# Hybrid decoder step on one core: the mixer's gate pairs summed on VectorE, and the sample output's steps moved apart

## The chip, the cores and the metric

The kernel runs on one core of a Trainium2 chip. The metric is the device time of one launch in microseconds (us), the median of several runs. The profile is one execution under the hardware profiler.

The core has TensorE (PE: matmuls; PEld is its weight load), VectorE (DVE), ScalarE (ACT) and GpSimd (POOL). SyncE (SP) issues most DMA transfers. Each engine runs its own queue of instructions in order and waits at the head of it.

## The reference

One layer of a hybrid decoder, all in float32, width 1024, on 512 prompt tokens, 16 meta tokens ahead of them and 8 x 4 sample tokens with a paged cache of 256 positions each:

```python
h = x + 0.5 * rms_norm(swiglu(rms_norm(x, ffn1_pre_g), ffn1_w_gate, ffn1_w_up, ffn1_w_down), ffn1_post_g)
u = rms_norm(h, mix_pre_g)
proj = u @ w_in                      # q_a, k_a, v_a, gk_low, r_a, q_b, k_b, v_b, gate_a, gate_b
...
o_a = rms_norm(o_a, gla_norm_g).reshape(B, L, V_GLA).astype(x.dtype) * jax.nn.silu(r_a)
...
    z = jnp.einsum('bqhd,bkhd->bhqk', qblk, k).astype(jnp.float32) * scale + bias_f
    l = jnp.where(mask, jax.nn.log_sigmoid(-z), 0.0)
    r = lax.cumsum(l, axis=3, reverse=True) - l
    a = jnp.where(mask, jnp.exp(jax.nn.log_sigmoid(z) + r), 0.0)
    return jnp.einsum('bhqk,bkhd->bqhd', a.astype(v.dtype), v)
...
m = jax.nn.sigmoid(gate_a) * (o_a @ w_o_gla) + jax.nn.sigmoid(gate_b) * (o_b @ w_o_sb)
h = h + rms_norm(m @ w_out, mix_post_g)
y = h + 0.5 * rms_norm(swiglu(rms_norm(h, ffn2_pre_g), ffn2_w_gate, ffn2_w_up, ffn2_w_down), ffn2_post_g)
```

The sample tokens attend over the cached keys and values as well; that is the "sample" work below. The mixer is the last third of the layer's middle: the products for r_a, gate_a and gate_b (columns of w_in) and the two output projections w_o_gla and w_o_sb.

## The kernel before

**Products.** Each float32 product is made of three fast ones: an operand is split into a high part (a cast on ACT to a shorter float, `S.copy` into `hi`) and a low part (`lo` = x - hi, on DVE), and PE adds hi*hi, hi*lo and lo*hi (L730 to L733 for a plain tile, L1081 to L1083 for a pair). Tokens lie in two halves of 280 and 264 columns.

**Tiles and pairs.** `MIXER` is the written list of the mixer's products. An "R" entry is a tile of 128 output columns, taken in 8 steps of six matmuls. An "S" entry is a pair: two neighbouring tiles of 128 columns made together by a scheme of seven products of half the size in place of eight (`seven_steps`), 14 steps. The order, with the step at which each begins in the part that concerns us: r 3 (8), r 5 (22), tiles o 0 and o 1 (36, 44), a 0 (52), o 2, b 0 (74), o 3, a 2 (96), o 4 (110), b 2 (118), o 5 (132), a 4 (140), o 6, b 4 (162), o 7, a 6 (184), b 6 (198), then the p products of w_o_sb. "a", "b" are gate_a, gate_b; "o" and "p" are w_o_gla and w_o_sb.

**What a pair needs of its weights.** The two 128-column blocks, cut in halves of their rows, give b11, b12, b21, b22 (the upper and lower half of the first and second block); sums of them are operands of the seven products. With "positive" pairs two raw tiles are fetched (two loads of 256 KB each): r1 = (b11 | t1's part) and r2 = (b22 | b21), and `weight_sums` makes four sums on DVE: t3 = b22 + t1, t1 = t1 + b11 (in place), t2 = b22 + t1, t4 = b21 + t2, each 128x512. The operands "b1" (r1), "t" (t2 | t3), "b2" (r2), "t4" are then split by `parts_of` (hi) and `parted_lo` (lo). After the low parts of b1 and b2 the next raw is fetched.

With "adding" pairs the sums t1 and t3 are made by transfers: `fetch` loads a third half from DRAM into a room (L654), and `Chunks.add` (L676) issues on POOL's queue a DMA that reads a block of w_in again and adds it onto the raw, or onto the room. `weight_sums` leaves out its first two sums. Before the change, the pairs b 0, b 2, a 4, b 4 and a 6 of the mixer are "adding"; r 3, r 5, a 0, a 2, b 6 and the p pairs are "positive". (Seven pairs of keys and values earlier in the kernel are "adding" too, and stay so.)

**What sets the order.** Nothing is reordered by a compiler: on PE, DVE, ACT and POOL the program's order is the order of the queues. `when(n, f)` puts f at step n of the mixer, and `later(d, f)` d steps after the present one. `weights_at(when, n, f, sums, b1, t, b2, t4)` puts a pair's work at offsets from its first step n. Its defaults are sums (-10, -10, -9, -8), b1 (-6, -5), t (-2, -1), b2 (0, 1), t4 (4, 6); the first number of a pair of them is the hi cast, the second the lo. SP issues transfers in program order, and waits for each one's buffer.

**Buffers.** Raw tiles come from three buffers (pool tag `raw`), hi and lo from pools of their own. All else lies in an arena of 150 units: `take` reads the next place from the table `PLACES`, a list of bytes written ahead for this very order of takes and gives, so a room's place says which older use a new one must wait for.

**The sample tokens' work** runs beside the mixer's products. For each half of the heads, `Weights.new` (L2254) makes 64 matmuls of 32 columns (new tokens' scores), `sigmoids` (ACT, L2261 and L2262), `scan` (DVE, from a L176 on to L2268), `turn` (transposes on PE, L2278 and L2279), `out` (DVE). The V cache is loaded by SP in the same stretch (L2159). At the end `sample_out(i)`, i = 0 to 3, takes the sample output out: 0 copies the accumulator to SBUF (ACT, L2331), 1 transposes it on PE (L2336, four matmuls), 2 and 3 copy it in 8 pieces of 64x32 each (ACT, L2344) into the rooms `ob[0..3]` and `ob[4..7]`, beside the prompt's output. From step 122 on, `o_sums(i)` makes sums of `ob[i]` and `ob[i + 4]` on DVE for the p pairs.

In `seven_steps` two copies on ACT (L1071, `S.copy(b, a)` after two steps and `S.copy(c, b)` after six) start one accumulator from another: PE needs the first at the fourth step, the second at the eighth. Copies to rooms are L1061.

Of the kernel before, what the change touches and what calls it, by code (L numbers as in the profile page):

```python
# [16 lines left out]
P = 128  # L17
D = 1024
KD = D // P
# [11 lines left out]
C_QB, C_KB, C_VB, C_GA, C_GB = 3088, 4112, 5136, 6160, 7184  # L31
# [12 lines left out]
MIXER = [("R", "r", 0), ("R", "r", 1), ("R", "r", 2), ("R", "r", 7), ("S", "r", 3), ("S", "r", 5)]  # L44
# [6 lines left out]


PLACES = bytes.fromhex("""
063048361456185a44461e8c909270287c767e869488842c8a682478807a66028e0050726a263c646074823b555e6e0e522a10206c620c4e0220
421c3c3e2e401f050256545a3814161218583a7a7836662026726a80000464828e602a740e4e520a086c066e622e3432303d4a0c867e2c948a24
905e5c280e1c705a5118689289487c761f8c844a0323220240204f0f0d501c4392421a3c1f481823687d004c9302763f21518852201a42921f49
224e4a02687c487d3f504118884b7793001c761f4992047c0242483e684b7d931a18231f8892767c0002774804413e40681a7d20923f7c768800
1f204941404b68047d203e77767c92881f414b404921482316687c7692903a6662585e6c6a385c1f06366e44607294308a8e2474802c3e40122e
143c484c6e4e1c182a4400122d42201f146088184a432c1244616088892a1412431315126088891415121360614e18002634126061133c0c6854
0f1124123136847c563e3a2d0d6e5862387a8832424a4c4434302f786c8a74601272066a945d697d634159108c080a667092903f27373b85576f  # L60
0e1f2b3d552a215c606422828e49762c122e80488624137e281474261f5a5c8a6c15215e5d124978796a6b1494668c08125c72069248210a901c
30707804024e1868506a16521a36237a62843e016e7c543c560e0c5789882a920610402b59005a1c2102045e423e0e2248084e703a6233121432
7a5c57946e7c8966780c928884855a4c4a1f01009030561c7a8c72125c1052045e581636211a14034018026e787c2a62942b8988686657436a44
51400a0608343000425a323c84908c724e4a5b126e7850011f21703e7c7a7b94621a0e1b22566a922a84031e484643444c8c908868381c54183a
4a583c5b6e7866727c1a707a163e4f1f0c0148441158561e1b36124a144c434e1601223e18381f48014f0c551e4c4a1454224421183a5246501f
11434e58123e361b564601480c1f44361112544e181c501458564f1748524a4c211e3e3a01430c124e201154365646481e4a181c44573e385943
1612044c4e51143e0154360c1620591252115614504e5446484a1c181e0d0f4c580c3e0401433739563e01124f0d4c564520224e1636383a464a
14121b1848100d540c1e0104433e524e4c16010d1f37543658434556524c50100e124a1c1814460c3a374e3e044816211f4c384354014f3e0c1f
483638181c3a2256583e4c0e4a1052541e464e5c505e524414124c563e583a0c06040121440803225e52424a107c3c161a5a22484c383a365654
1f3e505c4e1e060c7c5a46030e22205e361e4a3e585e524210403c03480e47201e4a5c50464e464c2220383a220c367c4e5a20060e4248524c46  # L70
5e220e0c4a03514420424c4e085c061e52024a450450010c225c5a085e52113032341e1000424e0a0e4c20065c0042225b34101e0c2330324e50
4c5a044a0a00235c200e220e425a44024c205c5d42005a0e200242004c5a23220f4c220e00545c121c7d565a7c38183e163514403a363c1a1e4c
005c56547c7d0c585b100e34325a7c62243084707a9064928c4e828a68788e2826942a6a5a6e677e72806b2c8671486c88465a004e702e607a74
7c6682766e80146a488c683092080a906240062570363a34842438203e1e193c2232574a8a651642460e4d541c18448a71242812101a0c644d25
86567e602e59293c3270574a241e6c78087a2a88293e38363a24210a74942c1e2334408a84299062282421682d072b06698c92257b09617f0b89
7c28766d79952f7214248e6a80764a8264660e306e421e20226218460c12901070325b371c92163c00023e8a84344056504e8c047494867a7e78
5c60087c5a5e2d25543b2a293606586c681846594d454a424f887c08521d51503a2c243627584c5456064e442a4d591d4a4225180a3a581c3808
4f5054283b4e562e4a44264d24192a1c4c50361829284e1a0b384a57250a46582b504419182455264e38360b0a574c284f502a194647244a1854
3a454e44384c374f0a194753242a184655544456383a50364e526a8e5c7678648662248a80180a7470823c60021e7a00547e6e06342c94841090
423208302e18265424284a2a06744c4d3034274b294a2a264d284c32304c2927264b4d4a283042064a41181b401e1c207426281a5c1c026a223e  # L80
3c8a
""")


# [53 lines left out]
def hybrid_step(  # L138
# [15 lines left out]
    V, S, G, T = nc.vector, nc.scalar, nc.gpsimd, nc.tensor  # L154
# [64 lines left out]
    r = 0  # L219
# [50 lines left out]
    win = w_in[0]  # L270
# [1221 lines left out]
    st = Chunks([])  # L1492
# [12 lines left out]

    def gate_weights(w, c):
        a, b = w[:, c : c + P], w[:, c + P : c + 2 * P]
        plain = c < C_GA + 4 * P or c == C_GB + 6 * P if w is win else True
        kind = "positive" if plain else "adding"
        return [((a, b), 0, KD, 0, P, kind), ((b, a), 4 * P, KD, 0, P, kind)]  # L1510

    for kind, what, n in MIXER:
        w, c = {"r": (win, C_RA), "a": (win, C_GA), "b": (win, C_GB), "o": (w_o_gla[0], 0), "p": (w_o_sb[0], 0)}[what]
# [5 lines left out]
    with tc.manual_schedule(engines={E.PE, E.DVE, E.Activation, E.Pool}):  # L1519

        w, r0, kt, c0, nw, kept = st.todo.pop(0)
# [70 lines left out]
        for j in range(2):  # L1592
            c = slice(P * j, P * j + P)
# [203 lines left out]
        p = ps()  # L1797
        for j in range(5):
            n = P if j < 4 else NTL
# [713 lines left out]
    with tc.manual_schedule(engines={E.PE, E.DVE, E.Activation, E.Pool}):  # L2513
        kps, mixer_at, at = {}, {}, {}

        def when(n, f, *args):
            mixer_at.setdefault(n, []).append((f, args))
# [389 lines left out]
```

## Time and profile before

| | us |
|---|---|
| median of 3 runs (1492.51 to 1493.57) | 1493.03 |
| the profiled execution | 1491.81 |
| its span | 1490.1 |
| TensorE busy | 1472.3 (99%) |
| VectorE busy | 1100.3 (74%) |
| ScalarE busy | 812.8 (55%) |
| GpSimd busy | 72.6 (5%) |
| granted TensorE clock, mean | 0.999 |
| bytes moved | 196.13 MB, 132 GB/s |

The span is from the first to the last instruction. TensorE is busy nearly throughout, so the time changes only where TensorE's few gaps do: what matters is which engine or transfer ends each of them. A row of the timeline has the start, the length, engine, line and operation, and in brackets the idle time before it and what ended it.

### The profile page before, as it was taken

How to read it: one execution, taken by the hardware profiler on the slowest of the kernel's cores; microseconds unless marked ns; L12 is line 12 of the kernel's file. 1: busy time of each engine (PE TensorE's matmuls, PEld its weight loads, DVE VectorE, ACT ScalarE, POOL GpSimd, SP SyncE). 2: the span in 40 equal slices, each digit the busy share in tenths (PEclk: the TensorE clock that was granted, in tenths of full speed). 3: DMA queues.
4: the chain of work that ended last, by engine and by line, in shares of the span. 5: the costliest groups of instructions: out<-in, count | busy, mean ns of one | idle time of the engine just before them, and what ended most of it. 6: DMA issues, size and time to landing. Idle time of an engine off the chain costs nothing.

```text
span 1490.1 us, 29979 instructions
## 1 busy us (share of the span) xinstructions
PE 1472.3 (99%) x11881; PEld 1419.6 (95%) x11881; DVE 1100.3 (74%) x1856; ACT 812.8 (55%) x1527; POOL 72.6 (5%) x193
## 2 busy tenths in 40 slices
PE   9999999999999999999999999999999999999998
PEld 8999999999899899889988989899999999999998
DVE  5888888854677865888877755668667898888554
ACT  7455445533555655767766553565564455455333
POOL 2000000000000012201100010100000000000000
PEclk9999999999999999999999999999999999999999
DMA  8133333224665687467677887866531333333252
GB/s 253 50 93 100 100 93 104 84 79 124 174 143 136 164 175 151 100 127 150 145 142 187 215 161 211 192 156 179 169 106 56 100 100 100 99 105 94 79 176 92
DMA packets 298829, 196.13 MB, mean 132 GB/s; under 512 B 11548, under 2 KB 274914, under 8 KB 298690
## 3 DMA queue, kind: packets, MB, share of 16 engines
q1 hardware_dynamic: 285714, 187.87, 47.4%
q0 software_dynamic: 12960, 6.36, 4.0%
q8 instruction: 93, 1.52, 0.4%
q14 instruction: 46, 0.38, 0.1%
q10 hardware_dynamic: 16, 0.00, 0.0%
HBM read 166.86 MB, written 27.33 MB: 130 GB/s over the span
## 4 chain that ended last, share of the span: by engine, by line
PE 51%; DMA 4%; DVE 3%; ACT 1%; issue 1%; SPq 0%; DVEq 0%; POOLq 0%
PE acc L1302 4%; PE acc L1303 4%; PE acc L1304 4%; PE acc L1081 3%; PE acc L1083 3%; PE acc L1082 3%; DMA raw<-in_w_in_dram 3%; PE acc L743 3%; PE acc L746 3%; PE acc L744 3%; PE acc L730 2%; PE acc L733 2%; PE acc L731 2%; PE ps L2116 1%; PE ps L2001 1%; PE ps L2100 1%
## 5 line engine op out<-in xcount | busy, mean ns | idle before, releaser
L173 DVE TENSOR_TENSOR room<-room,room 128x560 fp32r<-128x560 f32 (+15 forms) x486 | 304.0, 646 | 77.0 <-ACT room L810 12.9
L173 DVE TENSOR_TENSOR lo<-raw,hi 128x1024 fp32r<-128x1024 f32 (+1 forms) x207 | 248.0, 1199 | 87.4 <-ACT hi L1008 59.9
L1302 PE MATMUL acc<-room,hi 128*128 128x280 f32 (+1 forms) x896 | 259.6, 290 | 0.0
L1304 PE MATMUL acc<-room,lo 128*128 128x280 f32 (+1 forms) x896 | 259.4, 290 | 0.0
L1303 PE MATMUL acc<-room,hi 128*128 128x280 f32 (+1 forms) x896 | 259.1, 289 | 0.0
L1008 ACT CAST hi<-raw 128x1024 fp32r<-128x1024 f32 x118 | 124.0, 1055 | 144.7 <-PE acc L1303 58.0
L1304 PEld LDWEIGHTS acc<-room,lo 128*128 128x128 f32 x896 | 168.7, 188 | 0.0
L1303 PEld LDWEIGHTS acc<-room,hi 128*128 128x128 f32 x896 | 168.7, 188 | 0.0
L1302 PEld LDWEIGHTS acc<-room,hi 128*128 128x128 f32 x896 | 168.4, 188 | 0.0
L1081 PE MATMUL acc<-room,hi 128*128 128x280 f32 (+1 forms) x532 | 158.5, 298 | 1.7 <-ACT acc L1071 1.5
L730 PE MATMUL acc<-room,hi 128*128 128x280 f32 (+1 forms) x544 | 155.9, 303 | 0.3 <-DVE room L176 0.3
L1083 PE MATMUL acc<-room,lo 128*128 128x280 f32 (+1 forms) x532 | 154.3, 290 | 1.1 <-DVE lo L173 1.1
L1082 PE MATMUL acc<-room,hi 128*128 128x280 f32 (+1 forms) x532 | 154.2, 290 | 0.0
L731 PE MATMUL acc<-room,hi 128*128 128x280 f32 (+1 forms) x544 | 147.1, 290 | 0.0
L173 DVE TENSOR_TENSOR lo<-room,hi 128x1024 fp32r<-128x1024 f32 x110 | 104.9, 954 | 49.8 <-ACT hi L1008 49.8
L1008 ACT CAST hi<-room 128x1024 fp32r<-128x1024 f32 x110 | 92.5, 841 | 87.8 <-PE acc L1303 60.4
L708 ACT CAST hi<-raw 128x1024 fp32r<-128x1024 f32 (+1 forms) x89 | 89.4, 1004 | 78.6 <-issue 19.2
L733 PE MATMUL acc<-room,lo 128*128 128x280 f32 (+1 forms) x544 | 113.1, 289 | 0.0
L743 PE MATMUL acc<-room,hi 128*128 128x280 f32 (+2 forms) x388 | 110.9, 295 | 0.2 <-ACT hi L708 0.2
L744 PE MATMUL acc<-room,hi 128*128 128x280 f32 (+2 forms) x388 | 108.9, 290 | 0.0
L743 PE MATMUL acc<-room,room 128*128 128x280 f32 (+3 forms) x368 | 108.4, 295 | 0.0
L730 PEld LDWEIGHTS acc<-room,hi 128*128 128x128 f32 x544 | 103.1, 190 | 5.0 <-issue 3.5
(407 smaller groups left out, 3563.0 us busy)
## 6 DMA issues: line engine op xcount, KB each, us to landing
raw<-in_w_in_dram SPq DMA_DIRECT2D x68, 256.0 KB, 5.1
raw<-in_ffn_w_gate_dram SPq DMA_DIRECT2D x64, 256.0 KB, 3.3
raw<-in_ffn_w_up_dram SPq DMA_DIRECT2D x64, 256.0 KB, 3.2
raw<-in_ffn_w_down_dram SPq DMA_DIRECT2D x36, 448.0 KB, 3.7
raw<-in_w_in_dram SPq DMA_DIRECT2D x29, 512.0 KB, 7.4
out_dram<-room SPq DMA_DIRECT2D x36, 256.0 KB, 6.1
room<-in_cache_k_dram SPq DMA_DIRECT2D x32, 256.0 KB, 7.4
room<-in_cache_v_dram SPq DMA_DIRECT2D x32, 256.0 KB, 6.9
```

What stands on the lines that cost most here:

```text
L173: (eng or V).tensor_tensor(out=out, in0=a, in1=b, op=op)
L730: T.matmul(acc[h][:, :w], hi[k], act.get(k, h, w)[0], start=(k == order[0]), stop=False, skip_group_check=True)
L731: T.matmul(acc[h][:, : wid[h]], hi[k], a[h][1], start=False, stop=False, skip_group_check=True)
L743: T.matmul(acc[h][:nw, : wid[h]], wh, a[h][0], start=(k == 0), stop=False)
L744: T.matmul(acc[h][:nw, : wid[h]], wh, a[h][1], start=False, stop=False)
L1008: S.copy(hi[:, :kt], src)
L1081: T.matmul(x[:, :n], hi, act_[k][0][:, :n], start=(first and k == 0), stop=False, skip_group_check=True)
L1082: T.matmul(x[:, :w], hi, act_[k][1][:, :w], start=False, stop=False, skip_group_check=True)
L1083: T.matmul(x[:, :w], lo, act_[k][0][:, :w], start=False, stop=(k == 3), skip_group_check=True)
L1302: T.matmul(x[:, :QW], hi, act[k][0], start=(first and k == 0), stop=False, skip_group_check=True)
L1303: T.matmul(x[:, :QW], hi, act[k][1], start=False, stop=False, skip_group_check=True)
L1304: T.matmul(x[:, :QW], lo, act[k][0], start=False, stop=(k == 3), skip_group_check=True)
```

## The change

All pairs of `gate_weights` become "positive": for b 0, b 2, a 4, b 4 and a 6 the third load and the two adding transfers go, and the first two sums are made on DVE. All mixer pairs now use the default offsets of `weights_at`. The steps of `sample_out` change from 1, 4, 7, 9 to 1, 5, 9, 11 after step 112. The table `PLACES` is replaced as a whole, since the order of takes and gives is another; its rows are left out here.

```diff
     def gate_weights(w, c):
         a, b = w[:, c : c + P], w[:, c + P : c + 2 * P]
-        plain = c < C_GA + 4 * P or c == C_GB + 6 * P if w is win else True
-        kind = "positive" if plain else "adding"
-        return [((a, b), 0, KD, 0, P, kind), ((b, a), 4 * P, KD, 0, P, kind)]
+        return [((a, b), 0, KD, 0, P, "positive"), ((b, a), 4 * P, KD, 0, P, "positive")]
...
             if kind == "S":
-                behind = MIXER[i - 1][0] == "S"
-                if what == "r" or (what == "a" and t < 4) or behind or (what, t) == ("p", 2):
-                    weights_at(when, n, (what, t), b1=(-4, -3) if behind else (-6, -5))
-                else:
-                    weights_at(when, n, (what, t), (-5, -5, -4, -3) if behind else (-6, -6, -5, -4), b1=(-4, -2) if behind else (-6, -5),
-                               t=(-2, 0) if behind else (-3, -1), b2=(0, 3), t4=(7, 9))
-                    for d in (-14, -9) if behind else (-16, -12):
-                        when(n + d, st.add)
+                weights_at(when, n, (what, t), b1=(-4, -3) if MIXER[i - 1][0] == "S" else (-6, -5))
...
         for i in range(4):
-            when(n + (1, 4, 7, 9)[i], sample_out, i)
+            when(n + (1, 5, 9, 11)[i], sample_out, i)
```

So a pair that was "adding" has its sums on DVE at -10 to -8 (two of four, at -5 and -4, before), its "t" at -2 and -1 (-3, -1), b2's low part and with it the next fetch at 1 (3), and t4 at 4 and 6 (7, 9). PE's instructions keep their order but for the four transposes of `sample_out`, one step later. DVE has ten instructions more, POOL ten adding transfers fewer, SP five loads fewer.

The order of the queues at three places. Names are tiles with running numbers; raw_... is a raw tile, room_... a place in the arena.

First SP, where the raws of pair b 0 are fetched. Before (raw_10342 and raw_10407 are r1 and r2, the load between them the third half):

```order
L2159 DMA room_134_9400<-in_cache_v_dram 128x512
L2159 ISA
L2159 DMA room_92_5271<-in_cache_v_dram 128x512
L206 DMA raw_10306<-in_w_o_gla_dram 128x8x128
L646 DMA raw_10342<-in_w_in_dram 128x4x128
L647 DMA raw_10342<-in_w_in_dram 128x4x128
L654 DMA room_103_5553<-in_w_in_dram 128x4x128
L646 DMA raw_10407<-in_w_in_dram 128x4x128
L647 DMA raw_10407<-in_w_in_dram 128x4x128
```

After (raw_10335 and raw_10400; x2 are the two halves; lines behind `gate_weights` are two lower than before, so L2157 is L2159):

```order
L2157 DMA room_93_5274<-in_cache_v_dram 128x512
L2157 ISA
L2157 DMA room_98_5529<-in_cache_v_dram 128x512
L206 DMA raw_10299<-in_w_o_gla_dram 128x8x128
L663 DMA raw_10335<-in_w_in_dram 128x4x128 x2
L2157 ISA
L2157 DMA room_100_5550<-in_cache_v_dram 128x512
L663 DMA raw_10400<-in_w_in_dram 128x4x128 x2
L2157 ISA
L2157 DMA room_71_4268<-in_cache_v_dram 128x512
```

The third load is gone, and a load of the V cache stands between the two raws in place of ahead of them.

Then DVE, where the sums of b 0 and the scan of the second half of the heads stand. Before (raw_10342, raw_10407 as above; the 128x544 rows are the end of an earlier product):

```order
L173 TENSOR_TENSOR lo_10508<-raw_10306,hi_10507 128x1024
L173 TENSOR_TENSOR room_9_92<-room_134_9400,room_9_92 128x544
L173 TENSOR_TENSOR room_82_4594<-room_83_4677,room_82_4594 128x544
L173 TENSOR_TENSOR room_103_5553<-raw_10407,raw_10342 128x512
L173 TENSOR_TENSOR lo_10606<-raw_10342,hi_10605 128x1024
L173 TENSOR_TENSOR room_92_5271<-raw_10407,room_103_5553 128x512
L176 SCALAR_TENSOR_TENSOR room_83_4677<-room_83_4677,newm 128x32
L2267 TENSOR_SCALAR room_83_4677<-room_83_4677 128x32
L2268 SCALAR_TENSOR_TENSOR room_83_4677<-room_83_4677 128x288
```

After:

```order
L173 TENSOR_TENSOR lo_10499<-raw_10299,hi_10498 128x1024
L173 TENSOR_TENSOR room_91_5266<-raw_10400,raw_10335 128x512
L173 TENSOR_TENSOR raw_10335<-raw_10335 128x512
L173 TENSOR_TENSOR room_91_5266<-raw_10400,raw_10335 128x512
L173 TENSOR_TENSOR room_130_9726<-raw_10400,room_91_5266 128x512
L173 TENSOR_TENSOR room_98_5529<-room_9_113,room_98_5529 128x544
L173 TENSOR_TENSOR room_9_113<-room_91_5266,room_9_113 128x544
L173 TENSOR_TENSOR lo_10600<-raw_10335,hi_10599 128x1024
L176 SCALAR_TENSOR_TENSOR room_98_5529<-room_98_5529,newm 128x32
L2265 TENSOR_SCALAR room_98_5529<-room_98_5529 128x32
L2266 SCALAR_TENSOR_TENSOR room_98_5529<-room_98_5529 128x288
```

Four sums stand together ahead of the two 128x544, where two stood behind them, one on each side of b1's low part; they are followed by b1's low part and the scan.

Last ACT, around the start of pair b 2 and the sample output. Before (hi_11118 is the cast of b1, hi_11147 of t, hi_11174 of b2; ps_9847 the sample accumulator, ps_11156 its transposes):

```order
L1008 CAST hi_11118<-raw_10898 128x1024
L2331 COPY room_83_4677<-ps_9847 128x512
L1008 CAST hi_11147<-room_9_92 128x1024
L1008 CAST hi_11174<-raw_10951 128x1024
L2483 COPY room_78_4275<-acc_11103 128x280
L2483 COPY room_78_4275<-acc_11104 128x264
L2344 COPY room_80_4319<-ps_11156 64x32 x2
L2344 COPY room_103_5553<-ps_11156 64x32 x2
L2344 COPY room_134_9400<-ps_11156 64x32 x2
L2344 COPY room_103_5553<-ps_11156 64x32 x2
L1071 COPY acc_11179<-acc_11177 128x280
L2344 COPY room_80_4319<-ps_11156 64x32 x4
```

After (hi_11111, hi_11144, hi_11165 and t4's hi_11212; ps_9842 and ps_11154; the second L1071 comes next behind these rows and four more L2342; L2329 is L2331 of before, L2342 L2344, L2481 L2483):

```order
L1008 CAST hi_11111<-raw_10890 128x1024
L2329 COPY room_122_8264<-ps_9842 128x512
L1008 CAST hi_11144<-room_75_4401 128x1024
L1008 CAST hi_11165<-raw_10943 128x1024
L2481 COPY room_71_4268<-acc_11096 128x280
L2481 COPY room_71_4268<-acc_11097 128x264
L1071 COPY acc_11170<-acc_11168 128x280
L2342 COPY room_93_5274<-ps_11154 64x32 x2
L2342 COPY room_122_8264<-ps_11154 64x32 x4
L2342 COPY room_49_872<-ps_11154 64x32 x2
L1061 COPY room_49_872<-acc_11169 128x280
L1008 CAST hi_11212<-room_100_5550 128x512
```

The first L1071 stands ahead of all sixteen pieces, where it stood behind eight; the t4 cast now stands between the two eights.

More of the change, by code (lines that the diff above doesn't have):

```diff
@@ L53 @@
 PLACES = bytes.fromhex("""
[L54 to L81, printed above, removed]
+4806001e1a382b1422241862847c7e583c0e328e667a74763e646e786a70544f8a12820c308c269456806c5a368868424486465c34721090265b
+926052504e405a2726383a142c365c5e26545a2e2a6a78190c708c301e126c94568a8280424a483486728890684010080a50014e60063e747a92
@@ new lines @@
+0e663c584364846e8f4a2612176213151c763202511a0163484450647e1e7c43121d8e4613264b53421c04001a4e4945521f62024412204d8e43
+7c1c1726044c4b421e19484e6252538f494417267c208e214c424b12501b0405481e5326165221208e4e7c4a621b050448147d50122926288e20
+274a161b04054862294a507c287d8e522713121b04162926544a7c484c828e880a9074687a0c7850808c66222708365a92703c302c5610725846
+128a6a660e001b1942441e28511d4e561958461262275719434647272919424557281c44421c29282744454647425a1e3c40621c052784080c06
+646c6204012c102a8e0a7a520e13128a6600583002341c04328251726e80165761944070744a0f6d112b8b51907c2d3e14524e3c37072f0d0b8f
@@ new lines @@
+65785009853b57277e3948686a4d886228368c497686299278196e72561a278060484a4c284929957119277c3c48287a124a7494703e82444020
+421e465064585a52004e225e5c8e19908a1494272e2c2a165510060885846d70120e0c6c4c260a8254301a20643e7a1e505814086c90024a2c03
+947c19103c70854806462e848b8a40743456264d0a824c1a94307c54420e5e271c4a226429900c022c3c2010704838528e8b8584405b215a824e
+5d08010a140603004d0516122c7c8a94443c26183e904c7a0c29488e706d6c5674301e31242a826c5866105a2c1c11202e4e94547c5250403234
+3e3c1248706484908e3b7a8a221e250c435b1c18422c2a115030203e3c2e245a400c221e52321c2c435b0c25113e2a18243c2e4032345c5e221c
@@ new lines @@
+4142205a282c52301e2a0c433c252218245a1c2e52505e44201e2f4126465c28100c425a1e313c2a5c241c1a182f46424432505230100d34411d
+2c285e2a1e212e28183c0d5b34205a2c240c3c2e26403e44461e5052425e325c301d182a1a280d0f26405b2a18313c245a200c302e2c100e3422
+2a1e505232463e4442415c5e302e181b28200c435b3c2c5a24261118281a302a2246445052423e1e3c1d412c0e2e103331200c3c5b18242e0e30
+1e343250522c0c2e5a205e2a284244224846493e3c10244b181a26405a0a0c42205c2e5e28145f102c12402a248e4b0c0e0a301e32262234103a
+054a0842445f3c205a2c463f5e8e300a3e34124a1c0a462a404c370524445e32221e083e5f128e42262648325e3c30345a20122c440a248e422a
@@ new lines @@
+40265e3c054447085a450a3c8e222e5e422c20445c120514281e263e402e471606225e420001453c8e5a0826420a0544141e224500281601065e
+12205a3c5c472c088e8f000a062004422c448e8f0806000a202c020042478e44060a008e420806104c47181c444a3a52501534483230370e1e22
+1914060c181b088e1d0a44464228168a947890125e92767274197e7a6a7c704e86626c815464806e8c668312168882608440182454896814667e
+2a2e2c805e745c6482728a92946a5a407a3e3c3390760a888679104a0c4c8e42380048308f912004021e5308223a468e7891790e36064451534e
+5a146e12667e78004248383391307c6a1660686c900c4c104a787670628c843091860a8e88907a403c3d4e5c79785d61178a902c6f6d6763158d
@@ new lines @@
+762a727f7d138592803c746472322c5e30941e3420005008523a4240382236067a4e0d484c1a188a24901c28860a88540c588e265a686a768c70
+5c62124660667e48047c8584163d016e6c425441572f0f0c11787e123f7d2d562a4c2c023d00847c4a48470e580185462e4241142a3c13120244
+043d0c0084464a5441567c852f2c16142e0110003c3e462a4a0c1205843d2c407d562e7c1716003e030e4a0585470c3c84562c7d7c0412162e0e
+02462f470c0085564a8404057c122d2c46472e020e0c841064908c867a34323a208a583670562c041c740662685a28305224882e7650724c4a48
+427c6a144e54402a523e163c007612133e4f3c4e3d7c12516a7d6b3e504f3d7d6b7c4e6a3c5a54064e45403d44047c4202006a3c32884a707c76
@@ L82 @@
+3e46
 """)
```

## The prediction

> **What bounds the kernel now.** I read the page first, then the mixer's stretch by window, then the waits of TensorE there. The mixer's gate pairs, which the change touches, run from about 780 to 1060 us.
>
> ```profile
> span 1490.1 us, 29979 instructions
> PE 1472.3 (99%) x11881; PEld 1419.6 (95%) x11881; DVE 1100.3 (74%) x1856; ACT 812.8 (55%) x1527; POOL 72.6 (5%) x193
> ...
> 780.00:1060.00 280.00, 273.53 (x2512) 262.20 (x2511) 187.25 (x315) 151.93 (x295) 20.36 (x54) 0.99 0.74 183
> ...
> PE ps L2254 <- issue: 2.0, 1, 2.0
> PE ps L2336 <- ACT room L2331: 1.8, 1, 1.8
> PE acc L1081 <- ACT acc L1071: 1.5, 2, 1.2
> PE ps L2278 <- DVE room L176: 0.9, 1, 0.9
> PE acc L1081 <- ACT room L1061: 0.2, 1, 0.2
> ```
>
> TensorE (PE) is the bound: 1472.3 of 1490.1 us, so all its gaps together are 17.8 us. The window's columns are length, then busy time of PE, weight load, VectorE (DVE), ScalarE (ACT), POOL, then clock, DMA share and GB/s. In the mixer PE is idle 280.00 - 273.53 = 6.5 us, and the five waits name 2.0 + 1.8 + 1.5 + 0.9 + 0.2 = 6.4 of it. Only these can be won here: neither fewer bytes nor fewer POOL instructions shorten PE. VectorE is busy 187 of 280 us and has room for more. The change adds no matmul, so the question is which of the five waits it touches, and what new ones it makes.
>
> **Wait 1, L2254 (2.0 us), and the slow clock behind it.** This is the last part of a burst of 64 tiny matmuls of one half's new-token scores.
>
> ```profile
> 882.51 0.73 PE L2254 MATMUL ps<-room,room 128*32 128x32 f32 x61
> 885.26 0.25 PE L2254 MATMUL ps<-room,room 128*32 128x32 f32 x3 [2.03 <-issue]
> ...
> 861.80:883.00 21.20, 21.20 (x255) 20.36 (x256) 9.41 (x12) 10.89 (x22) 4.06 (x6) 1.00 0.93 132
> 885.40:888.80 3.40, 3.40 (x17) 3.36 (x16) 0.00 (x0) 0.47 (x2) 0.00 (x0) 0.51 1.13 292
> ...
> q0 software_dynamic: 309, 0.16, 92.3%
> q8 instruction: 1, 0.02, 2.4%
> ...
> q8 instruction: 20, 0.33, 0.5%
> ```
>
> PE stops after matmul 61 of 64 and waits for no semaphore. Queue q8 (rows: packets, MB, share of the 16 DMA engines) carries PE's instructions: in the mixer 20 packets serve 2512 + 2511 matmuls and loads, 251 each. Between 861.8 and 883.0 PE used 255 + 256 = 511, two packets' worth; the next packet is in the stretch 882.5 to 885 (the row with one). In that stretch q0, POOL's adding transfers, occupies 92.3% of the DMA engines. I read the stop as a late instruction packet behind crowded DMA engines. After it the granted clock is 0.51 for 3.40 us, which costs 3.40 x 0.49 = 1.67, say 1.6 us. So the place costs 2.0 (2.1 with the matmuls' own spacing) + 1.6 = 3.7 us.
>
> [...]
>
> **Wait 2, L2278 (0.9).** DVE and PE, then SP's and POOL's issues and their landing times (the last column), around gate pair b0:
>
> ```profile
> 882.33 1.44 DVE L173 TENSOR_TENSOR room<-room,room 128x544 f32<-128x544 f32 x2
> 889.42 0.69 DVE L173 TENSOR_TENSOR room<-raw,raw 128x512 f32<-128x512 f32 x1 [5.66 <-DMA raw<-in_w_in_dram]
> 890.50 1.23 DVE L173 TENSOR_TENSOR lo<-raw,hi 128x1024 fp32r<-128x1024 f32 x1 [0.39 <-ACT hi L1008]
> 892.25 0.19 DVE L176 SCALAR_TENSOR_TENSOR room<-room,newm 128x32 f32<-128x32 f32 x1
> 894.16 0.41 PE L2278 MATMUL ps<-ident,room 128*128 128x128 f32 x2 [0.91 <-DVE room L176]
> ...
> 871.57 0.50 SPq L647 DMA_DIRECT2D raw<-in_w_in_dram  x1
> 874.81 1.27 POOL L676 DMA_DIRECT2D raw<-in_w_in_dram  x1 [31.35 <-DMA raw<-in_w_in_dram]
> ...
> raw<-in_w_in_dram SPq DMA_DIRECT2D x2, 256.0 KB, 11.9
> raw<-in_w_in_dram POOLq DMA_DIRECT2D x1, 256.0 KB, 14.6
> ```
>
> DVE stands 5.66 us at the head of its queue for the first adding transfer (issued 874.81, landed 14.6 later at 889.4); behind it stand b1's low part and the scan (L176 on) that L2278 needs. PE's excess there is 1.1 us.
>
> **Waits 3 to 5, around pair b2 and the sample output.** ACT, then PE:
>
> ```profile
> 932.70 1.04 ACT L1008 CAST hi<-raw 128x1024 fp32r<-128x1024 f32 x1 [4.32 <-DMA raw<-in_w_in_dram]
> 933.65 0.58 ACT L2331 COPY room<-ps 128x512 f32<-128x512 f32 x1
> 936.36 1.05 ACT L1008 CAST hi<-room 128x1024 fp32r<-128x1024 f32 x1 [2.13 <-DMA room<-in_w_in_dram]
> 938.82 1.53 ACT L2344 COPY room<-ps 64x32 f32<-64x32 f32 x8
> 940.37 0.38 ACT L1071 COPY acc<-acc 128x280 f32<-128x280 f32 x1
> 940.77 1.54 ACT L2344 COPY room<-ps 64x32 f32<-64x32 f32 x8
> 943.27 0.63 ACT L1008 CAST hi<-room 128x512 fp32r<-128x512 f32 x1
> ...
> 936.29 0.29 PE L1081 MATMUL acc<-room,hi 128*128 128x280 f32 x1
> 940.80 0.40 PE L1081 MATMUL acc<-room,hi 128*128 128x280 f32 x1 [1.25 <-ACT acc L1071]
> 942.78 0.39 PE L1081 MATMUL acc<-room,hi 128*128 128x280 f32 x1 [0.17 <-ACT room L1061]
> ```
>
> The same chain in ACT: b1's cast waits 4.32 us for a sum landed by the adding transfer, and the copy L2331 behind it lets the transposes L2336 start 1.8 us late (2.0 with spacing). The t cast then waits for the second adding transfer until 936.36; b2's cast, eight L2344 and only then L1071 follow, so PE waits 1.25 at 940.80 and a little at 942.78: 1.4 + 0.3 = 1.7 us.
>
> **The change, part by part.**
>
> ```profile
> 907.40 0.69 DVE L173 TENSOR_TENSOR room<-raw,raw 128x512 f32<-128x512 f32 x1
> 909.58 0.69 DVE L173 TENSOR_TENSOR room<-raw,room 128x512 f32<-128x512 f32 x1
> ...
> 898.96 1.32 SPq L663 DMA_DIRECT2D raw<-in_w_in_dram x2
> ...
> 919.56 1.28 POOL L676 DMA_DIRECT2D raw<-in_w_in_dram  x1 [35.47 <-DMA raw<-in_w_in_dram]
> 958.25 1.26 POOL L676 DMA_DIRECT2D raw<-in_w_in_dram  x1 [14.84 <-DMA raw<-in_w_in_dram]
> ...
> DMA to landing us min/median/max: 2.8/4.9/14.6
> ```
>
> Removed: per pair two adding transfers and one SP load, 3 x 256 KB, times five = 3.75 MB. All were off PE's path except through the waits above; POOL's 5 + 5 issues cost PE nothing by themselves.
>
> Added: two more sums per pair on DVE, 10 x 0.69 = 6.9 us. Cover: DVE's idle time, 280 - 187 = 93 us in the mixer. Pair a2 is already made this way: four sums from 907.40 to 910.27 with no gap, and none of PE's five waits lies at its products. If the cover goes, what stands behind the sums (b1's low part, scans) comes late. The sums now stand at steps -10 to -8 instead of -5, -4, where they need both raws. A step is six matmuls, about 0.77 us. For b2 and b4 POOL, which waits for the second raw, found it landed by 919.56 and 958.25; the sums' steps 108 and 152, counted from 936.29 and 942.78 (steps 118 and 124) with the wait at L2336 taken off the first, fall at about 926.6 and 964.3, 6 to 7 us later. For b0 it is tight: DVE is free for the sums at 882.4, and its second raw, issued at 871.57 and 11.9 us on the way, landed near 883.5; with the third load and the adding transfers out of the crowd I take the 8.4 us that a2 needed at most from issue to first sum (898.96 to 907.40): 880. One V cache load stands now between the pair's two raws in SP's queue: by the order its room is let go by transposes ahead of b0's low-part releases, so the second raw still goes out about 871; were that room late, so were this raw and the four sums, one for one.
>
> Then b0 on DVE: four sums 882.4 to 885.2, two 128x544 to 886.7, b1's low part to 887.9, scan (1.9 us from L176 to what L2278 needs, 892.25 to 894.16) done near 889.8. PE without wait 1 is at L2278 near 893.2 - 3.7 = 889.5. So wait 2 leaves 0.3: a gain of 0.8. (With wait 1 still there it goes whole.)
>
> Fetches come two steps earlier, since b2 and t4 are split earlier; a raw is let go sooner, which costs nothing where SP's queue isn't blocked.
>
> Sample output: copy at 113, transposes at 117 (were 116), copies at 121 and 123 (119, 121). The four transposes move six matmuls later, which by itself gives L2331 0.77 us more, and b1's cast ahead of it no longer waits for a transfer: wait 3 goes, 2.0. With t and b2 cast on time, the first L1071 runs as soon as PE lets it, since it stands now ahead of all L2344. But ahead of the second L1071 stand 8 copies, L1061, the t4 cast and 8 copies: 1.55 + 0.4 (a copy like L1071's) + 0.63 + 1.55 + 0.38 = 4.5 us, begun after the first L1071 about 1.9 us past b2's first matmul (two steps and 0.38) and due at 6.2 (eight steps). That ends at about 6.45: 0.3 us, and up to 1 if casts run late; I take 0.5. The last eight copies now also wait for DVE, whose sums of the first pair of outputs (step 122) now stand ahead of them and use a room that they write; by the same count DVE is done with them at 4.1, before ACT comes there at 4.5. So waits 4 and 5 give 1.7 - 0.5 = 1.2.
>
> All rooms get new places, so SP's transfers wait for other releases throughout the program. No row shows a price: by PE's idle outside the mixer (17.8 - 6.5 = 11.3 us, little to win) and the largest wait above (2.0), I bound it at -1 to +2 and take +0.3, near nothing, as most of PE's gaps were not on rooms.
>
> Sum: -3.7 - 0.8 - 2.0 - 1.2 + 0.3 = -7.4, say -7.5 us. The profiled execution took 1491.81 (span 1490.1 and 1.7 around it), so 1484.3; the median of the runs is 1493.03, 1.2 above, so 1485.5.
>
> **Rivals.**
> - *Wait 1 stays.* The V cache loads remain and crowd the engines too (0.93 DMA share from 861.8), so the packet may still be late, or the stop has another cause. Then wait 1 and its clock stay, wait 2 goes whole: -1.1 - 2.0 - 1.2 + 0.3 = -4.0, 1489. For it: only part of the crowd goes. Against: q0's 92.3% just there.
> - *No change.* The new rooms or the ACT queue between the two L1071 give back what waits 3 to 5 won (3.2 us), and wait 1 stays: about 1492. For it: ACT has 0.3 us less than it needs there already.
> - *Slower: the sums wait for raws and hold DVE.* Landing takes 4.9 us in the middle and 14.6 at most. At a2 the sums began 8.4 us after the issue of 898.96; at 14.6 they would be 6.2 late. What is behind them has 5 steps, 3.9 us, of slack, so it decides from a lateness of 3.9 on; five pairs x 2.3 = 11.5 us, less the 8 won: 1496.5. Against: the two rows of POOL, 6 us ahead. [...]
>
> **How the numbers follow.** The forecast 1485.5 has 0.47 (own range 1483 to 1487.5), the late packet 1489 0.25, no change 1492 0.15, slower 1496.5 0.09, still faster than 1483 (other gaps close too) 0.04. A measurement tells about 0.2%, 3 us, from no change: faster is below 1490.0, slower above 1496.0. Faster: 0.47 + 0.04 + four fifths of 0.25 = 0.71; slower 0.09; the rest 0.20. The range 1483 to 1492 leaves out 0.04 below and half of no change with slower above.
>
> **What would show it.** No wait of PE at L2254 and no clock near 0.5 there; DVE's four sums of b0 without a gap near 882; no adding transfer's wait in ACT ahead of the copy of the sample output; PE at the transposes without a wait; at most 0.5 to 1 us at the second L1071. It is wrong if the packet of q8 comes late in the new order, if DVE waits at a first sum, or if SP waits for rooms where it did not.

## The result, and the profile after

The changed kernel takes 1482.71 us in the median (1482.39 to 1483.45, 6 runs), the kernel before 1493.13 beside it: a ratio of 0.9935, 95% interval 0.9922 to 0.9947, so it is faster by 10.4 us. The forecast was 7.5 less, 1485.5, with a range from 1483.0: the time lies 0.3 us below its lower end (0.9935 of the median that the forecast started from, 1493.03, is 1483.3, just inside). All runs of the changed kernel lie within 2 us; those of the kernel before reached from 1488.6 to 1499.0 over the experiments.

The page and the mixer's stretch of the changed kernel, then its waits of TensorE there:

```profile
span 1480.7 us, 29952 instructions
PE 1470.9 (99%) x11881; PEld 1419.5 (96%) x11881; DVE 1106.6 (75%) x1866; ACT 812.1 (55%) x1527; POOL 57.9 (4%) x183
...
780.00:1060.00 280.00, 279.57 (x2578) 269.28 (x2577) 200.00 (x335) 159.18 (x310) 7.34 (x44) 1.00 0.64 175
...
PE acc L1081 <- ACT acc L1071: 0.3, 1, 0.3
```

PE's idle time in the mixer went from 6.5 to 0.4 us. The one wait left is not a new one: it is in a p pair, at 992.0 (1002.5 before), and made up 0.3 of the 1.5 listed for L1071 before. DVE does more (200 us in place of 187), and costs nothing by it.

Pair b0 in the changed kernel, PE and then DVE; L2252 is L2254 of before:

```profile
880.48 0.46 PE L2252 MATMUL ps<-room,room 128*32 128x32 f32 x32
880.76 0.49 PE L2252 MATMUL ps<-room 128*32 128x32 f32 x32
881.18 0.40 PE L730 MATMUL acc<-room,hi 128*128 128x280 f32 x1
...
880.28 0.68 DVE L173 TENSOR_TENSOR room<-raw,raw 128x512 f32<-128x512 f32 x1
881.00 0.69 DVE L173 TENSOR_TENSOR raw<-raw 128x512 f32<-128x512 f32 x1
881.72 0.69 DVE L173 TENSOR_TENSOR room<-raw,raw 128x512 f32<-128x512 f32 x1
882.45 0.69 DVE L173 TENSOR_TENSOR room<-raw,room 128x512 f32<-128x512 f32 x1
883.06 1.35 DVE L173 TENSOR_TENSOR room<-room,room 128x544 f32<-128x544 f32 x2
884.33 1.22 DVE L173 TENSOR_TENSOR lo<-raw,hi 128x1024 fp32r<-128x1024 f32 x1
885.46 0.18 DVE L176 SCALAR_TENSOR_TENSOR room<-room,newm 128x32 f32<-128x32 f32 x1
```

All 64 tiny matmuls run without a stop, and no bracket stands in DVE's rows: the raws have landed, and sums, low part and scan follow each other at once. ACT around pair b2 and the sample output:

```profile
921.57 1.04 ACT L1008 CAST hi<-raw 128x1024 fp32r<-128x1024 f32 x1
922.51 0.59 ACT L2329 COPY room<-ps 128x512 f32<-128x512 f32 x1
...
929.34 0.38 ACT L1071 COPY acc<-acc 128x280 f32<-128x280 f32 x1 [0.18 <-PE acc L1083]
929.63 1.53 ACT L2342 COPY room<-ps 64x32 f32<-64x32 f32 x8
...
931.47 0.62 ACT L1008 CAST hi<-room 128x512 fp32r<-128x512 f32 x1
932.00 1.52 ACT L2342 COPY room<-ps 64x32 f32<-64x32 f32 x8
933.54 0.38 ACT L1071 COPY acc<-acc 128x280 f32<-128x280 f32 x1
```

The cast and the copy behind it wait for nothing, where the cast waited 4.32 us; the first L1071 waits for PE and not PE for it. The second ends at 933.92, and PE starts its next matmul at 933.97, 0.40 after the one before, where its matmuls stand 0.13 apart: 0.27 lost.

Matching the two traces matmul by matmul, the time between them changes at these places:

```
where (time before)                        us
597.9  transposes L2043                  -1.35
603.0  L1083, first split of a pair      -1.13
858    burst of L2221 and L2308          -0.36
885.3  L2254                             -2.14
885.4 to 888.8  slow clock               -1.50
894.2  L2278                             -1.04
934.3 to 935.5  transposes L2336         -2.03
940.8, 942.8, 944.6  around L1071        -1.54
all the rest (+0.56 in the first 8 us)   +1.5
last matmul                              -9.7
```

### The profile page after: what moved, and what is told of

Its sections match the earlier page's. It is cut to its first block, busy times and chain, and to the rows that moved or that the text cites. A ratio compares the mean times of both kernels' runs of the same rounds, so it can differ in the third digit from the quotient of the medians.

```text
span 1480.7 us, 29952 instructions
## 1 busy us (share of the span) xinstructions
PE 1470.9 (99%) x11881; PEld 1419.5 (96%) x11881; DVE 1106.6 (75%) x1866; ACT 812.1 (55%) x1527; POOL 57.9 (4%) x183
## 4 chain that ended last, share of the span: by engine, by line
PE 94%; DVE 2%; ACT 2%; DMA 1%; issue 1%; DVEq 0%; ACTq 0%; SPq 0%
PE acc L1304 8%; PE acc L1303 8%; PE acc L1302 8%; PE acc L743 7%; PE acc L746 6%; PE acc L744 6%; PE acc L730 5%; PE acc L1081 4%; PE acc L731 4%; PE acc L733 4%; PE acc L1083 4%; PE acc L1082 4%; PE acc L1244 2%; PE acc L1241 2%; PE acc L1242 2%; PE ps L2114 1%
## 5 line engine op out<-in xcount | busy, mean ns | idle before, releaser
L173 DVE TENSOR_TENSOR room<-room,room 128x560 f32<-128x560 f32 (+12 forms) x484 | 300.9, 642 | 83.1 <-ACT room L810 17.7
L1083 PE MATMUL acc<-room,lo 128*128 128x280 f32 (+1 forms) x532 | 154.2, 290 | 0.1
```

What stands on the lines that cost most here:

```text
L173: (eng or V).tensor_tensor(out=out, in0=a, in1=b, op=op)
L1083: T.matmul(x[:, :w], lo, act_[k][0][:, :w], start=False, stop=(k == 3), skip_group_check=True)
```

## The experiments

**Which part of the change does it?** First each part was undone or done alone: the steps of the sample output, and the places.

The changed kernel with the old steps:

```diff
-            when(n + (1, 5, 9, 11)[i], sample_out, i)
+            when(n + (1, 4, 7, 9)[i], sample_out, i)
```

> The changed kernel with the sample output's steps of before (113, 116, 119, 121), all else as changed. Theory A (the adding transfers made the waits, the steps are worth little): PE has no wait at the transposes, since b1's cast no longer waits for a transfer; at most 1 us of wait at the L1071 copies, which stand behind eight pieces again. Time 1482.7 to 1483.7. Rival B (the moved steps carry the 3.6 us of waits 3 to 5): 1486 to 1486.5, with a wait of about 1.8 us at the transposes.

Measured: 1483.32 us (1483.11 to 1483.46), ratio to before 0.9932 (0.9911 to 0.9953). No wait at the transposes; two small ones of b2 come up beside the old one:

```profile
PE acc L1081 <- ACT acc L1071: 0.6, 2, 0.3
PE acc L1081 <- ACT room L1061: 0.2, 1, 0.2
```

So the steps are worth 0.6 us by the medians and 0.9 by the matched traces, and the rest comes without them: theory A.

The other way round, the kernel before with the new steps alone (the same line, reversed):

> The kernel before with only the sample output's steps moved (113, 117, 121, 123). Theory A: b1's cast still waits for the adding transfer ahead of the copy of the sample output, so the wait at the transposes only shrinks by one step, 0.77 us, to about 1.0, and the first L1071 gains up to 1.2 since it no longer stands behind eight pieces: 1491 to 1492.5. Rival B: the steps alone win the 3.6 us: 1489.5. Waits at L2254 (2.0) and L2278 (0.9) stay in both.

Measured: 1491.03 us (1488.88 to 1495.35), ratio 0.9991 (0.9977 to 1.0004): the interval holds no change and ends where rival B's value lies (1489.5 is 0.9977); the trace decides. Its waits in the mixer:

```profile
PE ps L2254 <- issue: 2.3, 1, 2.3
PE ps L2336 <- ACT room L2331: 1.4, 1, 1.4
PE ps L2278 <- DVE room L176: 0.8, 1, 0.8
PE acc L1081 <- ACT acc L1071: 0.8, 2, 0.5
```

The transposes still wait (1.4; 1.0 was expected), L1071 less (0.8). The waits at L2043 and L1083 near 600 us are gone here, though nothing was changed there, which the next two runs take up.

The changed kernel with the places of before (table replaced, 1561 of 1568 places as before):

```diff
-PLACES = ... the changed kernel's table
+PLACES = ... before's place wherever the same room is taken; free places for seven rooms of the plain pairs
```

> The changed kernel with the table of places of before wherever the same room is taken (1561 of 1568 takes; the seven rooms that the plain pairs take anew got free places). Theory A (two effects: the mixer's waits go with the adding transfers; the 2.5 us in the attention part, near 597 to 603 us, come from the new places): the mixer stays free of waits, the waits at L2043 (1.2) and L1083 (1.1) come back: 1485.2, between 1484.5 and 1486. Rival B (the attention part gained by chance of the run or through traffic, not by places): 1482.7. Rival C (the mixer's waits went by the places): 1488 or more.

Measured: 1481.64 us (1480.74 to 1484.22), ratio 0.9934 (0.9907 to 0.996). No wait near 600 us in this profile, against theory A's second half. What the places could change there is POOL's queue: a fill of a room (L1895, L1893 in the changed file) waits for that room, and an adding transfer stands behind it. The kernel before, then this run, with the landing time of that transfer, then the same transfer in the changed kernel:

```profile
579.40 1.22 POOL L1895 MEMSET room<- 128x1344 f32 x1 [15.41 <-DVE room L1955]
583.14 1.27 POOL L676 DMA_DIRECT2D room<-in_w_in_dram  x1
...
room<-in_w_in_dram POOLq DMA_DIRECT2D x1, 256.0 KB, 12.5
...
595.76 1.05 ACT L1008 CAST hi<-room 128x1024 fp32r<-128x1024 f32 x1 [2.41 <-DMA room<-in_w_in_dram]
```

```profile
578.75 1.22 POOL L1893 MEMSET room<- 128x1344 f32 x1 [14.72 <-PE ps L594]
...
room<-in_w_in_dram POOLq DMA_DIRECT2D x1, 256.0 KB, 8.3
...
593.24 1.08 ACT L1008 CAST hi<-room 128x1024 fp32r<-128x1024 f32 x1
```

```profile
575.35 1.26 POOL L676 DMA_DIRECT2D room<-in_w_in_dram  x1
```

In the first two the places and the issue are the same, near 583; the transfer took 12.5 us in the one and 8.3 in the other, and only 12.5 is too late for the cast. With the new places it goes out 8 us earlier, at 574.97 to 575.82 in all eight traces that have them. Nor was the wait the luck of one execution: the kernel with ten more transposes, further down, has the places of before, and L2043 and L1083 wait there again (1.4 and 1.1 us):

```profile
585.08 1.27 POOL L676 DMA_DIRECT2D room<-in_w_in_dram  x1
...
596.54 1.04 ACT L1008 CAST hi<-room 128x1024 fp32r<-128x1024 f32 x1 [2.55 <-DMA room<-in_w_in_dram]
```

Of five traces with the places of before two have the 2.5 us, of eight with the new places none. So the places set how early this transfer goes out, and with the old ones the execution decides whether it lands in time: theory A and rival B each have a part. The five times of this run lie in two groups, 1480.74 to 1481.64 and 1484.12 and 1484.22; that the upper two had the wait is not shown.

The kernel before with the new places (17 rooms of the mixer elsewhere):

```diff
-PLACES = ... the table of before
+PLACES = ... the changed kernel's place wherever the same room is taken
```

> The kernel before with the places of the changed kernel wherever the same room is taken (17 of 1568 elsewhere, all in the mixer). Theory A: the waits at L2043 and L1083 go, 2.5 us; the mixer's five waits and the slow clock behind L2254 stay: 1490.6, between 1490 and 1491.5. Rival B (no effect of places in the attention part): 1493. Rival C (places carry the mixer's waits): 1488 or less.

Measured: 1491.51 us (1489.15 to 1493.42), ratio 0.9989 (0.9974 to 1.0003), no measurable gain, though 2.5 us in two of five executions, 1 us in the mean, would lie inside the interval. There is no wait near 600 us, and the transfer there goes out at 575.31. In the mixer the stop at L2254 is absent, and the waits behind it have grown:

```profile
PE ps L2336 <- ACT room L2331: 3.0, 1, 3.0
PE ps L2278 <- DVE room L176: 2.5, 1, 2.5
PE acc L1081 <- ACT acc L1071: 0.3, 1, 0.3
...
890.10:893.50 3.40, 3.40 (x16) 3.34 (x17) 3.33 (x14) 1.05 (x3) 0.00 (x0) 0.53 0.70 187
```

The last row is the window behind L2278: a slow clock (0.53) follows this wait of 2.53 us as it followed the one of 2.03 at L2254. PE waits 2.5 + 3.0 us at two places here, and 2.0 + 0.9 + 1.8 at three in the kernel before.

**Pair b0 alone.** The kernel before with b0 plain, and the changed kernel with b0 adding:

```diff
-        plain = c < C_GA + 4 * P or c == C_GB + 6 * P if w is win else True
+        plain = c < C_GA + 4 * P or c in (C_GB, C_GB + 6 * P) if w is win else True
...
-                if what == "r" or (what == "a" and t < 4) or behind or (what, t) == ("p", 2):
+                if what == "r" or (what == "a" and t < 4) or behind or (what, t) in (("p", 2), ("b", 0)):
```

> The kernel before with pair b0 alone made plain (its four sums on DVE at -10 to -8, its places free ones), all other adding pairs and the sample output as before. Theory A: the waits at L2254 and L2278 and the slow clock go (about 4.7 us by the profile of before), the waits at L2336 and L1071 (3.5) stay: 1488.0, between 1487 and 1489.5. Rival B (the gain needs all five pairs' traffic gone): over 1490.5.

Measured: 1487.24 us (1483.54 to 1491.16), ratio 0.9961 (0.9946 to 0.9976), as theory A had it. Its waits in the mixer:

```profile
PE ps L2336 <- ACT room L2331: 1.6, 1, 1.6
PE acc L1081 <- ACT acc L1071: 1.2, 2, 0.9
PE acc L1081 <- ACT room L1061: 0.2, 1, 0.2
```

L2254 and L2278 are gone, what belongs to b2 stays.

```diff
-        return [((a, b), 0, KD, 0, P, "positive"), ((b, a), 4 * P, KD, 0, P, "positive")]
+        kind = "adding" if w is win and c == C_GB else "positive"
+        return [((a, b), 0, KD, 0, P, kind), ((b, a), 4 * P, KD, 0, P, kind)]
...
+                if (what, t) == ("b", 0):
+                    weights_at(when, n, (what, t), (-6, -6, -5, -4), b1=(-6, -5), t=(-3, -1), b2=(0, 3), t4=(7, 9))
+                    for d in (-16, -12):
+                        when(n + d, st.add)
```

> The changed kernel with pair b0 alone made by adding transfers again, at the steps of before (12 rooms placed elsewhere). Theory A: the waits at L2254 (in most runs) and L2278 come back, 1.0 to 4.7 us: 1484.5 to 1487.4; the transposes of the sample output and the L1071 copies stay as in the changed kernel. Rival B (no effect of one pair): 1482.7 to 1483.2.

Measured: 1486.09 us (1484.37 to 1486.75), ratio 0.9954 (0.9939 to 0.9969): some 3 us more than the changed kernel, inside theory A's bounds.

```profile
PE ps L2277 <- DVE room L176: 1.9, 1, 1.9
PE ps L2253 <- issue: 1.3, 1, 1.3
PE acc L1081 <- ACT acc L1071: 0.3, 1, 0.3
```

Both waits of b0 are back and no other.

**What stops PE at L2254?** Ten transposes were added to the kernel before, 65 us ahead of the stop:

```diff
             T.transpose(p[:NS, 256:384], beta[:, 256:], ident)
+            for _ in range(10 if self.c == 0 and q == 0 else 0):
+                T.transpose(p[:NS, 256:384], beta[:, 256:], ident)
```

> The kernel before with ten more transposes (128x128 out, the same result written again) in the sample work of the first half, some 65 us ahead of the stop: 20 more PE instructions in the stream, 1.3 us of PE time. Theory A (a packet of 256 instructions comes late): where PE stops at L2254 it stops ten matmuls earlier, after 51 of the 64 in place of 61, and the fetch begins that much earlier as well, so the time is 1493.1 + 1.3 = 1494.4 by the median or a little less. Rival B (the stop belongs to the instruction: its bank, its operands, a semaphore): it stops after 61 again. If there is no stop in the profile, this is open.

Measured: 1492.82 us (1489.96 to 1495.32), ratio 0.9995 (0.998 to 1.0011); the 1.3 us of added work don't show above the spread. The stop:

```profile
883.86 0.65 PE L2254 MATMUL ps<-room,room 128*32 128x32 f32 x51
886.64 0.32 PE L2254 MATMUL ps<-room,room 128*32 128x32 f32 x13 [2.13 <-issue]
937.88 0.66 PE L2338 MATMUL ps<-ident,room 128*128 128x128 f32 x4 [3.99 <-ACT room L2333]
```

PE stops after 51 matmuls, ten earlier: twenty instructions inserted ahead move the stop by twenty instructions (each matmul has a weight load: 11881 of each in the kernel before). It belongs to the place in the instruction stream, as a late packet of instructions has it, and not to the instruction. In this execution the transposes waited 3.99 us, more than twice as long as in the first profile.

Then the traffic of b0's adding transfers was put back into the changed kernel, into a room that nobody reads, so that neither DVE nor ACT waits for it:

```diff
+                    def crowd_room():
+                        crowd["r"] = r = take(KD * P)
+                        crowd["a"] = r.rearrange("p (k n) -> p k n", n=P)
+                        G.memset(crowd["a"][:, :4], 0.0)
+                        nc.sync.dma_start(crowd["a"][:, 4:], cx[2])
...
+                    when(n - 22, crowd_room)
+                    when(n - 16, lambda: G.dma_start(crowd["a"][:, :4], cx[0], accum_op=ALU.add))
+                    when(n - 12, lambda: G.dma_start(crowd["a"][:, 4:], cx[1], accum_op=ALU.add))
+                    when(n - 2, lambda: give(crowd.pop("r")))
```

> The changed kernel with the traffic of pair b0's adding transfers put back, and nobody waiting for it: one 256 KB load on SP and two 256 KB adding transfers on POOL's queue, of the same blocks of w_in at the same steps as before, into a room of their own that is not read (it takes no part in the result). Theory A (the stop at L2254 is a late packet of PE's instructions behind crowded DMA engines): the stop at the 64 tiny matmuls is back, 1 to 2.3 us, in the profile or, as it needs chance, in part of the runs, with the slow clock behind it where it is over 2 us: median 1483.5 to 1486.5, runs further apart than those of the changed kernel. No wait at L2278 over 0.3. Rival B (the stop came from DVE or POOL being held): no stop, 1482.7 plus at most 0.5.

Measured: 1484.48 us (1483.46 to 1485.77), ratio 0.9947 (0.9931 to 0.9963), but no stop in the profile; one wait of 0.4 at L2276. The profile fell on the fastest of the seven runs (1483.46; the others took 1484.27 to 1485.77, where theory A has them), so what the others met is not shown. The first adding transfer went out at 865.5, 9 us too early, since it had no raw to wait for. So once more with that wait:

```diff
+                    def crowd_add():
+                        G.tensor_copy(crowd["a"][:, 0, :1], st.raws[1][0][:, 7, :1])
+                        G.dma_start(crowd["a"][:, :4], cx[0], accum_op=ALU.add)
...
-                    when(n - 16, lambda: G.dma_start(crowd["a"][:, :4], cx[0], accum_op=ALU.add))
+                    when(n - 16, crowd_add)
```

> As the run with pair b0's traffic put back into a room that nobody reads, but the first adding transfer now goes out when it did before: POOL first copies one column of b0's first raw, so it waits for that raw to land (near 872) as the adding transfer had to. Theory A (crowded DMA engines make PE's packet of instructions late): the packet of q8 is over 400 PE instructions behind the one ahead of it (316 in the changed kernel, 514 before), PE stops 1 to 2.3 us near the end of the 64 matmuls, no wait for DVE over 0.5: median 1484.5 to 1486.5. Rival B (being held, not the traffic, made the stop): no stop, the packet at 300 to 370 instructions, median under 1484.

Measured: 1482.3 us (1482.12 to 1483.36), ratio 0.993 (0.9913 to 0.9948), and no stop in the list of waits. But the second half of the burst took 0.80 us in place of 0.49:

```profile
880.58 0.80 PE L2252 MATMUL ps<-room 128*32 128x32 f32 x32
```

The packets are those of queue q8, which the profile calls "instruction": 93 in the kernel before, one to 255.5 of PE's 2 x 11881 matmuls and weight loads. PE's instructions between the start of one packet's fetch and the next, the pair of fetches that ends at the burst, counted in the traces:

```
run                       fetch at   instructions   stop at the burst
after                       874.7        316          none
after again                 875.5        318          none
before, b0 plain            874.4        316          none
after, places of before     874.0        306          none
before, places of after     878.9        370          none
after, crowd                878.6        368          none
after, crowd timed          878.8        391          0.3
after, b0 adding            880.6        402          1.3
before, shifted             884.4        497          2.1
before                      883.0        514          2.0
before, new steps           881.3        514          2.3
```

Where b0's added traffic exists the packet is 50 to 200 instructions later. The count is taken where the fetch starts, and PE can run on from there: with b0 adding from 880.6 to 881.64, where it stops. If the matmuls and weight loads of each trace are numbered from its start, PE stops at one place in the stream: behind number 14149 (before, and with the new steps), 14148 (shifted, where that number falls ten matmuls earlier in the burst) and 14150 (b0 adding). That is 497 to 527 instructions behind the start of the fetch before. It goes on 2.2 to 2.4 us after the late fetch starts (883.04 to 885.26 in the kernel before).

With the crowd timed, the fetch starts at 878.75 and PE comes to number 14150 at 880.86: there its next instruction comes 0.27 us later, where neighbours stand 0.01 apart, at 881.13, which is 2.38 behind the fetch. With the places of after, 878.90 and 881.06 leave 0.04. In the rows at 306 to 318 the fetch starts over 6 us ahead of that place. So the late packet is shown, and the added traffic alone makes it late enough for a stop, though one of 0.27 us. That PE stops for want of these instructions is my reading of the one place of the stops; no row names it. What makes it 2.5 to 5.7 us later still than with the crowd timed in the three rows at 497 and above was not separated: they all have the adding transfers and the places of before together, and the places set when SP's loads of the V cache go out.

**What is left.** The last eight pieces behind the second L1071:

```diff
-            when(n + (1, 5, 9, 11)[i], sample_out, i)
+            when(n + (1, 5, 9, 13)[i], sample_out, i)
```

> The changed kernel with the last eight pieces of the sample output at step 125 in place of 123, behind the second L1071. Theory A: the last wait of the mixer's middle (0.3 us at the second L1071) goes: 0.3 us less than the changed kernel, 1482.4, too little to measure by the times and seen only in the trace. Rival B: the eight pieces then hold the copies behind them (L1061 and the casts of the next pair), and a wait of 0.3 to 1 us comes up there: 1482.7 to 1483.5.

> The changed kernel unchanged, for a comparison on the same chip: 1482.0 to 1483.5, the runs within 1.5 us of each other, no wait of PE in the mixer over 0.4 us.

Measured side by side: 1483.02 us (1482.3 to 1483.91) for the later pieces, 1482.71 (1481.61 to 1483.3; ratio to before 0.9929, 0.9911 to 0.9948) for the changed kernel again. The gap of 0.27 at b2 is gone from the trace, as theory A has it: the second L1071 now waits for PE,

```profile
933.52 0.38 ACT L1071 COPY acc<-acc 128x280 f32<-128x280 f32 x1 [0.32 <-PE acc L1083]
```

but the times do not tell it from nothing, so there is no better version to name.

The moved steps have a price that no time shows. The first sum of `o_sums(0)` (step 122) subtracts columns 280 to 559 of `ob[4]` from those of `ob[0]`, and the last eight pieces write columns 512 to 543 of `ob[4]`, those of the sample tokens. In the kernel before the pieces come first: they start at 940.77, and the sums behind them at 941.23 (first row). In the changed kernel the sums start at 930.44 (second row), and the pieces of `ob[4]` at 932.00:

```profile
941.23 0.81 DVE L173 TENSOR_TENSOR room<-room 128x280 f32<-128x280 f32 x2 [1.42 <-issue]
...
930.44 0.45 DVE L173 TENSOR_TENSOR room<-room,room 128x280 f32<-128x280 f32 x1 [0.59 <-ACT room L2342]
```

So with the new steps, and with 13 in place of 11 as well, this sum takes for the sample tokens what the room held before. The inputs of these runs hide it: the bias of these attention logits is near -48 (`sb_bias`, -6 times 8 in the reference), which leaves next to nothing of the sample output. With the old steps the order is right, so the version to keep is the one with the sums on DVE and the old steps, at 1483.32 us.

## Why the prediction was right or wrong, point by point

- **Wait 1 and the slow clock, -3.7:** -3.64 by the matched traces (2.14 + 1.50), right in size. Its cause was right in kind (a late packet: the stop keeps its place in the stream), too simple in one point: the added traffic alone gave a stop of 0.27 us, not of 2. PE stopped 497 to 527 instructions behind the start of the fetch before.
- **Wait 2, -0.8:** -1.04. The 0.3 left over was not there: DVE's two 128x544 took 1.35 us in place of 1.44, the scan 1.77 in place of 1.9, and it was done at 887.23, as PE came (887.37). That the sums at -10 cost nothing was right; b0's raws were there.
- **Wait 3, -2.0:** -2.03. The transfer alone held it: with the old steps there is no wait there either, so the moved step was not needed for it.
- **Waits 4 and 5, -1.2:** -1.54. The count gave 0.3 left, I took 0.5; 0.27 was measured. The row of 1.5 contained 0.3 of a p pair that nothing here touched. That the sums now stand ahead of the last eight pieces and read a room that these write was right, and it cost no wait; that the sums then read it too early was not seen.
- **Places, +0.3:** wrong in size and sign, and outside the bound of -1 to +2: -2.5 near 600 us in this pair of traces. The reason given, that most of PE's gaps were not on rooms, left out POOL's queue, where a fill that waits for a room holds an adding transfer: 583 with the old places, 575 with the new.
- **The sum, -7.4 against -10.4,** was short, in this pair of traces mostly outside the mixer. The mixer won 8.7 (the shift from 780 to 1060 us) where its waits were put at 7.7, the place near 600 us 2.5, and 1.5 was lost elsewhere. The times of this pair differ by 9.4, and the medians by 10.4: the profiled execution of the kernel before (1491.81) was one of the better half. The step behind it took the length of each wait from one execution. These waits end with adding transfers, and issue to landing differs from run to run: 12.6 to 14.7 us for b0's first, 13.1 to 14.4 for b2's first, 8.3 to 12.5 for the one issued near 583. The waits at the transposes were 1.4, 1.6, 1.8, 3.0 and 3.99 us in the traces with b2 adding, at L2278 0.8 to 2.5. The places-of-after run lost 2.5 + 3.0 us and slow clocks behind both without any stop at L2254. Against the changed kernel the mixer of the other traces with all pairs adding is 7.6 us longer (new steps), 8.4 (places of after) and 10.2 (shifted, without its added work). The narrow runs of the changed kernel fit this, as it has none of these transfers in the mixer. How the missing 3 us divide between the mixer and the place near 600 us in the median was not measured.
- The front matter says that SP issues in program order. The order of the calls is not kept: `fetch` asks for the second raw ahead of the third load, and in SP's queue and in the trace the load comes first (866.2, the raw 871.2).

The rivals: "wait 1 stays" did not happen; "no change" neither; the sums never waited for a raw in the changed kernel.

## What to carry to other kernels

An accumulating transfer can land at different times from run to run (8.3 to 12.5 us after one issue here); if an in-order queue stands behind it (DVE's for 5.66 us at b0), work on an engine with idle time can be cheaper, even though it adds instructions (here ten sums of 0.69 us). When a kernel's runs are spread far wider than its rival's, do not take the size of a wait from one profile: take two or three, or forecast the spread. A difference between two traces at a place that the change seems not to touch needs more than a third run: here one run without the wait spoke against the places, and only the issue times of all traces showed their part. And whoever moves a write to a later step looks for the reads that it passes, also where the results do not show it.

## What the runs showed of the hardware

The stops of PE here that show no semaphore go with one late packet of its instructions (251 to a packet in the mixer before, 20 packets for 5023). PE stopped at one place of its stream, 497 to 527 instructions behind the start of the fetch before, where the next fetch had started less than 2.2 us ahead (2.16 us gave a stop of 0.04, 2.11 us one of 0.27, 3.0 and 6 us none). And in these traces the slow clock (0.5, for 3.41 us) came after every wait within the kernel of 2.03 us or more (0.51 behind 2.03, 0.57 behind 2.13, 0.55 behind 2.32, 0.53 behind 2.53, 0.58 behind 3.99, 0.71 from 932.8 to 936.2 behind the 3.0 at L2336), and after none up to 1.95 (1.00 behind 1.32, 1.81 and 1.95). Windows of 3.4 us behind a wait, from the kernel with b0 adding (behind 1.32 and 1.95 us) and the shifted one (behind 2.13 and 3.99):

```profile
883.00:886.40 3.40, 3.40 (x27) 3.36 (x28) 0.00 (x0) 0.47 (x2) 0.00 (x0) 1.00 1.06 239
891.40:894.80 3.40, 3.40 (x28) 3.38 (x29) 3.33 (x14) 1.02 (x4) 0.00 (x0) 1.00 0.62 155
```

```profile
886.80:890.20 3.40, 3.40 (x28) 3.36 (x21) 0.00 (x0) 0.47 (x2) 0.00 (x0) 0.57 1.13 279
937.90:941.30 3.40, 3.40 (x18) 3.40 (x19) 1.96 (x3) 1.50 (x2) 0.00 (x0) 0.58 0.51 134
```

The clock is the third number from the end. So here a wait of 2.1 us cost 3.6 (2.14 + 1.50), and behind one of 1.95 the clock was 1.00, so no slow stretch came on top.
